# A time-mixing layer on one core: the first weight loaded between the halves of unit 0, and the scaling coefficients computed on rows

## The chip, the cores and the metric

The kernel runs on one core of one Trainium2 chip. The metric is the device time of one execution in microseconds; the time of a kernel is the median of its runs. The profile is one execution on the chip, taken by the hardware profiler; its span runs from the first to the last instruction.

## The reference

`x` has 16 sequences of 2048 tokens with 256 features each. Three per-feature mixing vectors and four 256 x 256 weights belong to it. Of these the key branch is computed by the reference and never used, so that the output is:

```python
x_prev[:, 1:, :] = x[:, :-1, :]          # the token before, zero for the first
xv = x * time_mix_v + x_prev * (1 - time_mix_v)
xr = x * time_mix_r + x_prev * (1 - time_mix_r)
v = xv @ value_weight
r = xr @ receptance_weight
out = (1 / (1 + np.exp(-r)) * v) @ output_weight
```

## The kernel before

**Tiling.** The work is cut into units of 512 tokens (`TU`), four of them in a sequence (`UB`), 64 in all. A unit holds four tiles (`UJ`) of 128 tokens; 256 features are two blocks (`KO`) of 128 partitions. For each unit TensorE transposes the tokens, so that the features lie on partitions (or a DMA transpose does it, for the last sequences). The transposed tokens stand in `xt`, where one more slot ahead of them holds the token before.

**The mixing.** The factor of a feature is moved into the weight: with `tms` = time_mix, `c_sb` = 1 / time_mix - 1 and the weight rows scaled by `tms`, the mixed input is `x + c_sb * x_prev` (`scale`, `add`). A zero in time_mix is replaced by 1e-30 first (line 241). For the receptance branch of unit 0 alone there is no mixing: `project_unmixed` adds up four products instead, two of the previous tokens with `w_prev` = weight * (1 - time_mix) and two of the tokens with the scaled weight `w_bf`.

**Per unit** follow the receptance product (`project` into `psum_r`), the sigmoid on ScalarE (`s_sb`), the value product (`psum_v`), the product of both on VectorE (`z_sb`), the output product (`psum_o`), and its copy and store. The main loop begins at line 646; the transposes of later units are put into it by `advance`.

**The order of the work** is written out by hand: each engine takes its instructions in the order in which the program names them, and only the semaphores between engines add to that. The start, which the change touches, runs like this:

- ScalarE's queue issues the two small loads of the mixing vectors into `tm_rows` (4 rows of 128, line 168). SP's queue issues, in this order, half 1 and half 0 of unit 0 (line 174), the receptance weight (line 180), half 1 and half 0 of unit 1, and the value weight (line 184). All six are 256 KB, in float32. Half 1 comes first since its last token column is the source of the shifted slot (line 309).
- GpSimd issues loads that cast to bfloat16: units 2 and 3 of sequence 0 (line 192), the first of them with a wait for the receptance weight; then the output weight (line 195) and sequence 1 in four pieces (line 152). Sequence 2 follows inside the loop (line 162).
- TensorE warms up on constants (line 204), transposes half 1 of unit 0 (line 300), then `tm_rows` (line 236, into a `psum_o` buffer), then half 0 in two parts of one tile, the second of them into the `psum_o` buffer again, and does a few more warm-up products.
- VectorE takes the four coefficients per partition out of PSUM (line 240) and works out `tms`, `tm_prev` and `c_sb` from them, five instructions on 128 x 4 elements (lines 241 to 249). Then it multiplies the first weight: `w_prev` (line 578, two instructions), the first block of `w_bf` (line 585). ScalarE does the second block (line 588), behind its copies of the transposed tokens (lines 305 and 309). Then VectorE mixes the value input of unit 0 (lines 354 and 376) and scales the value weight (line 594).
- TensorE's first products are those of line 398, then the transposes of unit 1 (line 272), the other half of `project_unmixed`, and the value product of unit 0 (line 384).

Of the kernel before, what the change touches and what calls it, by code (L numbers as in the profile page):

```python
# [8 lines left out]
FP32 = mybir.dt.float32  # L9
BF16 = mybir.dt.bfloat16  # L10
ALU = mybir.AluOpType
# [4 lines left out]
def kernel(  # L16
# [25 lines left out]
    nc = tc.nc  # L42

    B, S, D = x.shape
    P = 128
    KO = D // P
# [8 lines left out]
    H = UJ // 2  # L55
# [56 lines left out]
    loads = {}  # L112
# [51 lines left out]
    x_unit = opool.tile([P, 2, UJ, D], FP32, name="o_sb")  # L164
    tm_rows = consts.tile([2 * KO, P], FP32)
    w_f32 = consts.tile([P, 2, KO, D], FP32)
    for m, tm in enumerate([time_mix_r, time_mix_v]):
# [3 lines left out]

    def load_halves(e):
        for h in (1, 0):
            nc.sync.dma_start(  # L174
                out=x_unit[:, e, h * H : (h + 1) * H],
                in_=unit_rows(x, 0, e)[:, 0, h * H : (h + 1) * H, :],
            )

    load_halves(0)
    first_weight = nc.sync.dma_start(  # L180
        out=w_f32[:, 0], in_=receptance_weight.rearrange("(ko p) n -> p ko n", p=P)
    )
    load_halves(1)
    nc.sync.dma_start(out=w_f32[:, 1], in_=value_weight.rearrange("(ko p) n -> p ko n", p=P))
# [5 lines left out]
    x_first = xpool.tile([P, 2, UJ, D], BF16, name="x_bf")  # L190
    for e in (2, 3):
        op = nc.gpsimd.dma_start(out=x_first[:, e - 2], in_=unit_rows(x, 0, e)[:, 0])  # L192
# [36 lines left out]
    new_xt(0)  # L229
    tms = consts.tile([P, 2, KO], FP32)  # L230
    c_sb = consts.tile([P, 2, KO], FP32)
    tm_prev = consts.tile([P, 2, KO], FP32)

    def coefficients():
        ps = ps_o_pool.tile([P, 2, KO], FP32, name="psum_o")
        nc.tensor.transpose(
            out=ps.rearrange("p m k -> p (m k)"), in_=tm_rows, identity=ident_f[: 2 * KO, : 2 * KO]
        )
        tm = consts.tile([P, 2, KO], FP32)
        nc.vector.tensor_copy(out=tm, in_=ps)  # L240
        nc.vector.tensor_scalar(
            out=tms, in0=tm, scalar1=0.0, scalar2=1e-30, op0=ALU.is_equal, op1=ALU.mult
        )
        nc.vector.tensor_tensor(out=tms, in0=tms, in1=tm, op=ALU.add)
        nc.vector.tensor_scalar(
            out=tm_prev, in0=tm, scalar1=-1.0, scalar2=1.0, op0=ALU.mult, op1=ALU.add
        )
        nc.vector.reciprocal(c_sb, tms)
        nc.vector.tensor_scalar(out=c_sb, in0=c_sb, scalar1=-1.0, scalar2=None, op0=ALU.add)

# [44 lines left out]
    def first_transposes():  # L295
# [13 lines left out]
        nc.scalar.copy(out=xt[0][:, 0, :, 1:P], in_=ps[:, H - 1, :, 0 : P - 1])  # L309
        coefficients()  # L310
        part(0, 1, ps_v_pool, "psum_v")
        part(1, 1, ps_o_pool, "psum_o")

    def slots(piece, off=0):
# [260 lines left out]

    first_transposes()
    for ko in range(KO):
# [4 lines left out]
            scalar2=None,  # L582
# [166 lines left out]
```

## Time and profile before

| what | value |
|---|---|
| median of 3 runs | 199.56 us (198.65 to 200.79) |
| span of the profiled execution | 197.1 us; its own time beside the span isn't given |
| mean granted TensorE clock | 0.996 |
| busy TensorE / VectorE / ScalarE / GpSimd | 191.5 / 183.1 / 177.1 / 86.3 us |
| DMA moved | 58.13 MB, mean 295 GB/s |

How to read it: PE is TensorE's matmuls and PEld its weight loads, DVE is VectorE, ACT ScalarE, POOL GpSimd, SP the queue of SyncE; a `q` behind an engine is its instruction queue, as in SPq. L398 is line 398 of the kernel. In a timeline each row has its start, the time from the start of the first to the end of the last instruction that it merges, the engine, the line, the operation with its output and inputs, their shapes, and how many were merged; brackets hold the idle time of the engine ahead of it and whose work ended that. In the chain of waits a row is one link, with start and duration; "issue" is time in which nothing was waited for that the profile shows. In the table of DMA issues the last number is the time from the issue to the landing.

### The profile page before, as it was taken

Reading aid. Unit: us, or ns where it says so; the run is one execution under the profiler, and the core shown is the slowest. Engines: PE = TensorE matmul, PEld = TensorE weight load, DVE = VectorE, ACT = ScalarE, POOL = GpSimd, SP = SyncE. Lnnn points to the kernel's source line nnn. Section 1 sums busy time; section 2 is a strip of 40 time slices with the busy share of each in tenths; the row PEclk is TensorE's granted clock in tenths of the full one; section 3 lists DMA queues with packets and bytes.
Section 4 is the critical chain, followed back from the end, with each engine's and each line's share of the span. In section 5 each row is a group of like instructions: output and inputs, shape, how many; then the busy total and the mean of one; then the engine's idle time right before and its main releaser. Section 6 shows DMA issues by size and latency. Waiting matters only on the chain.

```text
span 197.1 us, 3735 instructions
## 1 busy us (share of the span) xinstructions
PE 191.5 (97%) x1358; PEld 123.0 (62%) x1364; DVE 183.1 (93%) x286; ACT 177.1 (90%) x197; POOL 86.3 (44%) x117
## 2 busy tenths in 40 slices
PE   8999999999999999999999999999999999999992
PEld 3556676666666666666666666666666666666660
DVE  0999999999999999999999999999999999999962
ACT  3699899999999999999999999999999999999982
POOL 2845542443665635624334266444433444444200
PEclk9999999999999999999999999999999999999998
DMA  5999999999999999999999999999999999999985
GB/s 185 238 176 224 218 254 262 247 259 262 296 413 283 283 296 332 283 238 198 376 209 290 335 346 186 212 218 241 290 290 419 419 421 419 416 416 421 382 327 221
DMA packets 35593, 58.13 MB, mean 295 GB/s; under 512 B 26004, under 2 KB 27128, under 8 KB 30840
## 3 DMA queue, kind: packets, MB, share of 16 engines
q1 hardware_dynamic: 31792, 41.34, 60.3%
q0 software_dynamic: 3632, 16.44, 41.6%
q8 instruction: 10, 0.16, 0.3%
q10 hardware_dynamic: 152, 0.13, 0.2%
q14 instruction: 7, 0.06, 0.1%
HBM read 34.34 MB, written 39.90 MB: 377 GB/s over the span
## 4 chain that ended last, share of the span: by engine, by line
PE 90%; DMA 6%; POOL 1%; issue 0%; SPq 0%; ACT 0%
PE psum_r L384 27%; PE psum_v L384 27%; PE psum_o L416 27%; PE ps_t L272 8%; DMA x_bf<-in_x_dram 4%; DMA w_f<-n_receptance_weight_dram 2%; PE ps_t L416 1%; POOL x_bf L192 1%; SPq L174 0%; POOL wo_bf L195 0%; PE psum_v L416 0%; POOL x_bf L152 0%; PE ps_t L384 0%; PE psum_r L416 0%; ACT x_bf L446 0%
## 5 line engine op out<-in xcount | busy, mean ns | idle before, releaser
L364 POOL TENSOR_SCALAR mix<-xt_both,c_sb 128x1024 bf16<-128x1024 bf16 (+1 forms) x55 | 61.1, 1110 | 85.5 <-DVE mix L376 82.3
L697 DVE TENSOR_TENSOR z_sb<-s_sb,psum_v 128x1024 bf16<-128x1024 bf16 (+1 forms) x64 | 76.8, 1201 | 2.3 <-PE psum_v L384 1.1
L376 DVE TENSOR_TENSOR mix<-mix,xt_both 128x1024 bf16<-128x1024 bf16 x112 | 76.8, 696 | 1.4
L384 PEld LDWEIGHTS <-w_bf 128*128 128x128 bf16 x512 | 48.5, 98 | 39.2 <-DVE mix L376 0.8
L658 ACT ACTIVATE s_sb<-psum_r 128x1024 bf16<-128x1024 f32 x63 | 65.2, 1034 | 6.2 <-PE psum_r L384 6.0
L384 PE MATMUL psum_v<-mix,w_bf 128*128 128x512 bf16 (+1 forms) x252 | 64.8, 378 | 0.4 <-DVE mix L376 0.2
L384 PE MATMUL psum_r<-mix,w_bf 128*128 128x512 bf16 x250 | 64.6, 379 | 0.2
L416 PE MATMUL psum_o<-wo_bf,z_sb 128*128 128x256 bf16 x486 | 63.2, 273 | 0.0
L416 PEld LDWEIGHTS <-z_sb 128*128 128x128 bf16 x512 | 52.0, 103 | 17.9 <-DVE z_sb L510 0.7
L471 ACT COPY o_sb<-psum_o 128x1024 f32<-128x1024 f32 x50 | 51.2, 1023 | 5.0 <-PE psum_o L416 4.8
L289 ACT COPY xt_both<-ps_t 128x1024 bf16<-128x1024 bf16 x32 | 32.9, 1039 | 0.0
L272 PEld LDWEIGHTS <-x_bf 128*128 128x128 bf16 x304 | 19.8, 98 | 8.4 <-DMA x_bf<-in_x_dram 0.4
L272 PE MATMUL ps_t<-ident,x_bf 128*128 128x128 bf16 x304 | 22.7, 219 | 0.2 <-DMA x_bf<-in_x_dram 0.2
L354 DVE TENSOR_SCALAR mix<-xt_both,c_sb 128x1024 bf16<-128x1024 bf16 (+1 forms) x47 | 21.3, 463 | 0.0
L638 ACT ACTIVATE mix<-xt_both,c_sb 128x1024 bf16<-128x1024 bf16 x14 | 16.3, 1163 | 0.0
L376 DVE TENSOR_TENSOR mix<-mix,xt_first 128x1024 bf16<-128x1024 bf16 x15 | 10.5, 708 | 0.1
L471 ACT COPY x_bf<-psum_o 128x1024 f32<-128x1024 f32 x10 | 10.2, 1015 | 0.0
L354 DVE TENSOR_SCALAR mix<-xt_first,c_sb 128x512 bf16<-128x512 bf16 x22 | 6.6, 350 | 0.3 <-ACT xt_first L282 0.2
L289 ACT COPY xt_first<-ps_t 128x1024 bf16<-128x1024 bf16 x6 | 6.0, 1022 | 0.0
L557 POOL COPY xt_first<-xt_first 128x254 bf16<-128x254 bf16 x5 | 2.0, 392 | 7.2 <-DVE mix L376 7.2
L162 POOL DMA_DIRECT2D x_bf<-in_x_dram x8 | 4.7, 584 | 0.0
L364 POOL TENSOR_SCALAR mix<-xt_first,c_sb 128x512 bf16<-128x512 bf16 x6 | 4.1, 685 | 1.3 <-DVE mix L376 0.8
(68 smaller groups left out, 52.3 us busy)
## 6 DMA issues: line engine op xcount, KB each, us to landing
out_dram<-o_sb SPq DMA_DIRECT2D x25, 1024.0 KB, 12.1
x_bf<-in_x_dram POOLq DMA_DIRECT2D x8, 1024.0 KB, 15.8
x_natural<-in_x_dram POOLq DMA_DIRECT2D x4, 1024.0 KB, 11.8
out_dram<-x_bf SPq DMA_DIRECT2D x4, 1024.0 KB, 14.4
x_natural<-in_x_dram POOLq DMA_DIRECT2D x4, 512.0 KB, 12.7
out_dram<-x_bf SPq DMA_DIRECT2D x4, 512.0 KB, 4.7
x_bf<-in_x_dram POOLq DMA_DIRECT2D x6, 256.0 KB, 7.0
o_sb<-in_x_dram SPq DMA_DIRECT2D x4, 256.0 KB, 3.9
```

The costliest lines, as they stand in the source:

```text
L162: return nc.gpsimd.dma_start(out=x_bf[b], in_=rows(b), max_dma_last_dim=run)
L272: nc.tensor.transpose(out=ps[:, jj], in_=src[:, jj, ko * P : (ko + 1) * P], identity=idn)
L289: nc.scalar.copy(out=xt[b][:, j0 : j0 + UJ], in_=ps)
L354: nc.vector.tensor_scalar(out=mixed(piece, ko), in0=tokens(piece, 0, ko), scalar1=c_sb[:, m, ko : ko + 1], scalar2=None, op0=ALU.mult,)
L364: op = nc.gpsimd.tensor_scalar(out=mixed(piece, 1), in0=tokens(piece, 0, 1), scalar1=c_sb[:, m, 1:2], scalar2=1.0, op0=ALU.mult, op1=ALU.mult,
L376: return nc.vector.tensor_tensor(out=mixed(piece), in0=mixed(piece), in1=tokens(piece, 1), op=ALU.add)
L384: nc.tensor.matmul(out=ps[:, mo, :], lhsT=w_bf[:, m, ko, mo * P : (mo + 1) * P], rhs=mixed((b, m, e * TU + lo, e * TU + hi), ko), start=(k ...
L416: nc.tensor.matmul(out=ps[:, j, :], lhsT=slot[:, ko, j], rhs=wo_bf[:, ko, :], start=(ko == 0), stop=(ko == KO - 1),)
L471: nc.scalar.copy(out=o[:, j0 : j0 + UJ, :], in_=ps)
L638: nc.scalar.activation(out=mixed(piece, ko), in_=tokens(piece, 0, ko), func=ACT.Copy, scale=c_sb[:, m, ko : ko + 1],)
L658: nc.scalar.activation(out=s_sb, in_=ps_r, func=ACT.Sigmoid)
L697: nc.vector.tensor_tensor(out=z_sb[:, :, c : c + n], in0=s_sb[:, :, c : c + n], in1=ps_v[:, :, c : c + n], op=ALU.mult,)
```

## The change

Three things are changed, all in the start.

- On SP's queue the receptance weight is issued between half 1 and half 0 of unit 0, no longer behind both.
- `tms` and `tm_prev` are computed on `tm_rows` itself, 4 rows of 128 (`row_s`, `row_prev`), ahead of the transpose. Then two small transposes, one for each, bring them to partitions, and one copy takes both out of PSUM (`coefs`, 128 x 8). Only the reciprocal follows at once; the subtraction of 1 that completes `c_sb` stands behind the scaling of the first weight.
- GpSimd's cast loads are issued by a function that is called after `first_transposes`; the first of them waits for the copy of the coefficients in place of the receptance weight.

```diff
+    coef_rows = [consts.tile([2 * KO, P], FP32, name=f"coef_rows{n}") for n in range(2)]
...
-    load_halves(0)
-    first_weight = nc.sync.dma_start(
+    load_half(0, 1)
+    nc.sync.dma_start(
         out=w_f32[:, 0], in_=receptance_weight.rearrange("(ko p) n -> p ko n", p=P)
     )
-    load_halves(1)
+    load_half(0, 0)
+    load_half(1, 1)
+    load_half(1, 0)
...
-    for e in (2, 3):
-        op = nc.gpsimd.dma_start(out=x_first[:, e - 2], in_=unit_rows(x, 0, e)[:, 0])
-        if e == 2:
-            tc.add_manual_dep(op.ins, first_weight.ins.name, SYNC, reason="behind the weight")
-    nc.gpsimd.dma_start(out=wo_bf, in_=output_weight.rearrange("(ko p) n -> p ko n", p=P))
-    load(1)
+
+    def cast_loads(after):
+        for e in (2, 3):
+            op = nc.gpsimd.dma_start(out=x_first[:, e - 2], in_=unit_rows(x, 0, e)[:, 0])
+            if e == 2:
+                tc.add_manual_dep(op.ins, after.ins.name, SYNC, reason="behind the first loads")
+        nc.gpsimd.dma_start(out=wo_bf, in_=output_weight.rearrange("(ko p) n -> p ko n", p=P))
+        load(1)
...
-    tms = consts.tile([P, 2, KO], FP32)
+    coefs = consts.tile([P, 2, 2, KO], FP32)
+    tms, tm_prev = (coefs[:, n] for n in range(2))
     c_sb = consts.tile([P, 2, KO], FP32)
-    tm_prev = consts.tile([P, 2, KO], FP32)
+    row_s, row_prev = coef_rows
+    nc.vector.tensor_scalar(
+        out=row_s, in0=tm_rows, scalar1=0.0, scalar2=1e-30, op0=ALU.is_equal, op1=ALU.mult
+    )
+    nc.vector.tensor_tensor(out=row_s, in0=row_s, in1=tm_rows, op=ALU.add)
+    nc.vector.tensor_scalar(
+        out=row_prev, in0=tm_rows, scalar1=-1.0, scalar2=1.0, op0=ALU.mult, op1=ALU.add
+    )
 
     def coefficients():
-        ps = ps_o_pool.tile([P, 2, KO], FP32, name="psum_o")
-        nc.tensor.transpose(
-            out=ps.rearrange("p m k -> p (m k)"), in_=tm_rows, identity=ident_f[: 2 * KO, : 2 * KO]
-        )
-        tm = consts.tile([P, 2, KO], FP32)
-        nc.vector.tensor_copy(out=tm, in_=ps)
...
+        ps = ps_o_pool.tile([P, 2, 2, KO], FP32, name="psum_o")
+        for n, row in enumerate(coef_rows):
+            nc.tensor.transpose(
+                out=ps[:, n].rearrange("p m k -> p (m k)"),
+                in_=row,
+                identity=ident_f[: 2 * KO, : 2 * KO],
+            )
+        op = nc.vector.tensor_copy(out=coefs, in_=ps)
         nc.vector.reciprocal(c_sb, tms)
-        nc.vector.tensor_scalar(out=c_sb, in0=c_sb, scalar1=-1.0, scalar2=None, op0=ALU.add)
+        return op
...
-    first_transposes()
+    cast_loads(first_transposes())
...
     nc.scalar.activation(
         out=w_bf[:, 0, 1, :], in_=w_f32[:, 0, 1, :], func=ACT.Copy, scale=tms[:, 0, 1:2]
     )
+    nc.vector.tensor_scalar(out=c_sb, in0=c_sb, scalar1=-1.0, scalar2=None, op0=ALU.add)
     scale(pieces(0)[1])
```

More of the change, by code (lines that the diff above doesn't have):

```diff
@@ L170, with load_half @@
         )
[L172 to L176, printed above, removed]
-            )
-    load_halves(0)
-    first_weight = nc.sync.dma_start(
+    def load_half(e, h):
+        nc.sync.dma_start(
+            out=x_unit[:, e, h * H : (h + 1) * H],
+            in_=unit_rows(x, 0, e)[:, 0, h * H : (h + 1) * H, :],
+        )
+    load_half(0, 1)
+    nc.sync.dma_start(
         out=w_f32[:, 0], in_=receptance_weight.rearrange("(ko p) n -> p ko n", p=P)
     )
-    load_halves(1)
+    load_half(0, 0)
+    load_half(1, 1)
+    load_half(1, 0)
     nc.sync.dma_start(out=w_f32[:, 1], in_=value_weight.rearrange("(ko p) n -> p ko n", p=P))
@@ L309, in first_transposes @@
         nc.scalar.copy(out=xt[0][:, 0, :, 1:P], in_=ps[:, H - 1, :, 0 : P - 1])
-        coefficients()
+        after = coefficients()
         part(0, 1, ps_v_pool, "psum_v")
         part(1, 1, ps_o_pool, "psum_o")
+        return after
     def slots(piece, off=0):
```

9 lines of the change are left out of this document (1 added, 8 removed).

## The prediction

> **What bounds the kernel now.** I read the page first: the engines' busy time and the chain that ended last.
>
> ```profile
> span 197.1 us, 3735 instructions
> PE 191.5 (97%) x1358; PEld 123.0 (62%) x1364; DVE 183.1 (93%) x286; ACT 177.1 (90%) x197; POOL 86.3 (44%) x117
> PE 90%; DMA 6%; POOL 1%; issue 0%; SPq 0%; ACT 0%
> ```
>
> TensorE is busy for 191.5 of 197.1 us and carries 90% of the chain. Another 7% of it is DMA and GpSimd, and the start is where one looks for that first. So the second view is the chain in order of time, over the first 25 us.
>
> ```profile
> 0.74 0.40 SPq L174
> ...
> 1.20 0.41 SPq L174
> ...
> 1.66 3.62 DMA w_f<-n_receptance_weight_dram
> 5.28 0.30 issue
> 5.58 0.74 POOL x_bf L192
> ...
> 6.33 0.55 POOL x_bf L192
> ...
> 8.12 7.37 DMA x_bf<-in_x_dram
> ```
>
> The receptance weight lands at 1.66 + 3.62 = 5.28. GpSimd, told to wait for it, begins its issues at 5.58: the two cast loads of unit 0's batch, then the output weight, then batch 1. The second load of batch 1, issued at 8.12, lands at 15.49. The chain then goes through TensorE without a long break, so what counts is when TensorE passes this point. The timeline there, and the two earlier waits of TensorE's path that matter, are the third view (start, duration, engine, line; in brackets the idle time before it and who ended it):
>
> ```profile
> 8.91 0.67 DVE L354 TENSOR_SCALAR mix<-xt_first,c_sb 128x512 bf16<-128x512 bf16 x2 [0.17 <-ACT xt_first L282]
> ...
> 12.10 0.55 PEld L384 LDWEIGHTS <-w_bf 128*128 128x128 bf16 x4 [0.42 <-DVE mix L376]
> ...
> 15.54 0.45 PEld L272 LDWEIGHTS <-x_bf 128*128 128x128 bf16 x8 [0.38 <-DMA x_bf<-in_x_dram]
> ```
>
> TensorE was ready at 15.54 - 0.38 = **15.16** and the data at **15.49**. Two chains meet here, 0.38 us apart: the load chain, which is late, and the compute chain, which has 0.38 us of slack. The compute chain can't win its slack back elsewhere: the wait at 12.10 is for VectorE's mixing, which itself began at 8.91 behind a ScalarE copy of TensorE's transposes of unit 1. A shift of those transposes therefore goes through to 15.16 one for one.
>
> **The start, row by row.** The fourth view is the timeline of the first 8 us.
>
> ```profile
> 3.66 0.98 PE L300 MATMUL psum_r<-ident_f,o_sb 128*128 128x128 f32 x4
> ...
> 4.57 0.23 PE L236 MATMUL psum_o<-ident_f,tm_rows 4*128 4x4 f32 x1
> 4.68 0.58 ACT L305 CAST xt_first<-psum_r 128x512 bf16<-128x512 f32 x1 [1.61 <-PE psum_r L300]
> ...
> 4.73 0.44 PE L300 MATMUL psum_v<-ident_f,o_sb 128*128 128x128 f32 x2
> 4.83 0.16 DVE L240 COPY tm<-psum_o 128x4 f32<-128x4 f32 x1 [3.96 <-PE psum_o L236]
> 5.03 0.17 DVE L241 TENSOR_SCALAR tms<-tm 128x4 f32<-128x4 f32 x1
> ...
> 5.05 0.44 PE L300 MATMUL psum_o<-ident_f,o_sb 128*128 128x128 f32 x2
> ...
> 5.23 0.16 DVE L244 TENSOR_TENSOR tms<-tms,tm 128x4 f32<-128x4 f32 x1
> 5.31 0.16 DVE L245 TENSOR_SCALAR tm_prev<-tm 128x4 f32<-128x4 f32 x1
> ...
> 5.42 0.39 ACT L305 CAST xt_first<-psum_v 128x256 bf16<-128x256 f32 x1
> 5.43 0.18 DVE L248 RECIPROCAL c_sb<-tms 128x4 f32<-128x4 f32 x1
> ...
> 5.65 0.17 DVE L249 TENSOR_SCALAR c_sb<-c_sb 128x4 f32<-128x4 f32 x1
> 5.68 0.41 ACT L305 CAST xt_first<-psum_o 128x256 bf16<-128x256 f32 x1
> 5.72 0.69 DVE L578 TENSOR_SCALAR w_prev<-w_f,tm_prev 128x256 bf16<-128x256 f32 x2
> 5.95 0.54 ACT L588 ACTIVATE w_bf<-w_f,tms 128x256 bf16<-128x256 f32 x1
> ...
> 6.14 0.73 PE L398 MATMUL psum_r<-xt_first,w_prev 128*128 128x512 bf16 x2 [0.26 <-ACT xt_first L305]
> 6.34 0.33 DVE L585 TENSOR_SCALAR w_bf<-w_f,tms 128x256 bf16<-128x256 f32 x1
> ...
> 6.60 0.65 DVE L354 TENSOR_SCALAR mix<-xt_first,c_sb 128x512 bf16<-128x512 bf16 x2
> ...
> 6.73 0.61 PE L398 MATMUL psum_r<-xt_first,w_bf 128*128 128x512 bf16 x2
> ...
> 7.17 1.04 PE L272 MATMUL ps_t<-ident_f,o_sb 128*128 128x128 f32 x8
> ```
>
> The first real product, at 6.14, was released by ScalarE's last copy of the transposed tokens (5.68 + 0.41 = 6.09), not by the weight: w_prev's first half (one of the two in 0.69 from 5.72) is done at about 6.07. Both inputs arrive within 0.02 us of each other; the later products of the group then wait for the scaled weights, the third until 6.73. The landing times come from the table of DMA issues, asked for one issue at a time (the last number is us from issue to landing); the row of queue 10, ScalarE's, is of the stretch 2.0 to 3.4 us.
>
> ```profile
> o_sb<-in_x_dram SPq DMA_DIRECT2D x1, 256.0 KB, 2.8
> ...
> o_sb<-in_x_dram SPq DMA_DIRECT2D x1, 256.0 KB, 3.4
> ...
> q10 hardware_dynamic: 4, 0.00, 0.3%
> ```
>
> Half 1 of unit 0 lands at 0.74 + 2.8 = 3.54, half 0 at 1.20 + 3.4 = 4.60, the weight at 5.28. The distances are 1.06 and 0.68.
>
> **Part 1, the weight between the halves.** One issue of 0.4 us and 256 KB changes places with another; no issue is added on SP's queue, and what follows (unit 1's halves, the value weight) keeps its place. All three are of one size, so I let the second in line land when the second did and the third when the third did: weight at 4.60 (0.68 earlier), half 0 at **5.28** (0.68 later). What the weight gains, the tokens lose, and the tokens released the first product. TensorE began 0.12 after half 1's landing (3.66), so it begins half 0 at 5.40. The first pair ends 0.44 later, at 5.84; the second pair starts 0.32 behind the first, as now (4.73, 5.05), at 5.72 and ends at 6.16. ScalarE copies the first pair from 5.88 and the second, 0.26 behind it (5.42, 5.68) but not before 6.18, for 0.41: the tokens are ready at **6.59**, the first product starts at 6.64, where it is 6.14 now. ScalarE's share of the weight scaling (L588), behind these copies, moves by the same half microsecond: from 6.45 to 6.99.
>
> **Part 2, coefficients on rows.** Three of VectorE's small instructions (L241, L244, L245: at 5.03, 5.23, 5.31, together 5.03 to 5.43) move ahead of the transpose, now on 4 rows. Both row vectors had been moved by 3.4 us, by queue 10's row, and VectorE is idle from its start to 4.83 (the 3.96 in brackets). Three instructions of 0.2 each end at about 4.0, ahead of the end of half 1's transposes (3.66 + 0.98 = 4.64): covered. If the rows came 0.6 us later, they would push the copy back one for one. The row shape (4 rows of 128) has no row in this trace; between 0.16 (these instructions) and 0.33 (L585, twice the width on all partitions), I take 0.2, and the cover holds at either end. Added on TensorE is a second small transpose, between 0 and 0.23 (L236's own, not overlapped); I take 0.2. So the copy starts at 5.03, twice as wide and still some 0.16, and ends at 5.19. The reciprocal follows 0.20 after its start, at 5.23, the w_prev products 0.08 behind that (as L245 behind L244): **5.31 instead of 5.72**, ready at 6.00; w_bf's first half at 6.26. The subtraction that finishes c_sb (0.17) moves behind them and ahead of the mixing of the value input (L354): that can start no earlier than the tokens, 6.64, where it starts at 6.60 now. VectorE's 0.41 is thus won and not used: the tokens are late next.
>
> The group's four products start at 6.64 and then every 0.22 (two take 0.61 or less, one of them 0.38): 6.86, 7.08, 7.30. The last needs ScalarE's weight half, ready at 6.99: no wait. Now the group has starts at 6.73 and 6.95 for its last two, since it waited. Unit 1's transposes follow at 7.52 instead of 7.17: **+0.35** for the compute chain, which reaches 15.16 + 0.35 = **15.51**. Bounds of this term: were half 0 to land as early as now, the chain would win about 0.1 (starts at 6.19, 6.41, 6.63, 6.85, none waiting); were the distance from weight to half 0 the 1.06 of the two halves, half 0 lands at 5.66 and the chain is 0.73 late.
>
> **Part 3, the cast loads behind the copy.** The wait moves from the weight's landing (5.28) to the copy's end (5.19). From the landing to the first issue passed 0.30; a wait for VectorE can cost between 0.05 and the same 0.30. So GpSimd begins at 5.24 to 5.49, 0.09 to 0.34 earlier than 5.58, and everything queued behind on GpSimd (two loads, the output weight, batch 1's four) moves along. If the transfers follow one for one, the data that TensorE waits for land at 15.15 to 15.40; if the DMA engines have no room, at 15.49 as now. TensorE starts 0.05 after landing: 15.20 to 15.54.
>
> **The sum.** TensorE starts the transposes at the later of 15.51 (compute) and 15.20 to 15.54 (load); now it is 15.54. That is **no change: -0.03 us**. From there TensorE runs to the end, so the span is 197.07. The profile gives no time of its own execution beside the span; the median of the runs, 199.56, lies 2.46 over the span, which nothing here changes. The forecast is 199.53, rounded **199.5**.
>
> **The rivals.**
> *A, the load chain decides.* If half 0 loses little by the swap, the compute chain is ready at 15.06 and the load chain's 0.09 to 0.34 is the gain: 199.2 to 199.5, middle 199.3. For it: the chain as it is drawn now goes through the weight and GpSimd, not through the tokens. Against it: 256 KB stand ahead of half 0 in one queue, and the first product waited for the tokens.
> The Trainium skill's page "SBUF — State Buffer", section "SBUF: two separate sides", says that GpSimd can't write the descriptors of its DMAs while VectorE runs an instruction that takes the shared port pair, as a scaling of SBUF data can. Here the two issues under VectorE's scalings took 0.74 and 0.55, so the trace allows 0.2 us of that; by the rule the earlier issues fall under the earlier w_prev scalings as they do now, and 0.2 of A's gain would be lost: 199.4.
> *B, slower: half 0 becomes the bound.* One mechanism: the tokens' transposes wait for half 0. It decides from the landing at which the compute chain passes 15.54, 0.03 later than I take, so from 5.31. At the distance of 1.06 (landing 5.66) the chain reaches 15.16 + 0.73 = 15.89: **+0.35**, 199.9; at 5.85, another 0.19: 200.1. For it: the trace has one distance of each size, and the transfer in the middle may be the slower for its shape. Against it: the last place in three ended at 5.28 whatever was in it.
> *C, the cast loads collide with the value weight.*
>
> ```profile
> 3.13 0.43 SPq L184 DMA_DIRECT2D w_f<-in_value_weight_dram  x1
> ...
> w_f<-in_value_weight_dram SPq DMA_DIRECT2D x1, 256.0 KB, 4.7
> ...
> 7.89 0.63 DVE L594 TENSOR_SCALAR w_bf<-w_f,tms 128x256 bf16<-128x256 f32 x2
> ```
>
> It lands at 7.83, and VectorE wants it at 7.89: 0.06 of cover. If the casts, 0.09 to 0.34 earlier, delay it by as much, VectorE is up to 0.28 late when it comes to the row at 8.91; but it waits 0.17 there now, and its input is 0.35 later after the change, so the delay is swallowed: 199.5.
> That the change doesn't do what it says is half of the forecast: w_prev is ready earlier, and nobody takes it.
>
> **How the numbers follow.** Forecast, with 0.15 us either way, 0.55; A 0.2; B 0.2; C 0.05. The mechanisms span -0.34 to +0.55: 199.2 to 200.1. The three runs of one kernel lie from 198.65 to 200.79, so a median carries some 0.6 us of its own; the range is **198.5 to 200.6**. No case comes near 1% (2.0 us, about what a measurement of this kernel can tell from no change), so only the runs' spread can: faster by more than that 0.04, slower 0.05 (B adds to it), within it 0.91.
>
> **What would show it.** Right: w_prev's multiplications start near 5.3; the copy of the last tokens ends near 6.6; the first product starts near 6.6, released by ScalarE, and the four follow without gaps; unit 1's transposes near 7.5; GpSimd's first issue near 5.3; the transposes of 15.54 within 0.15 of that. Wrong: half 0's transposes at 4.8 (then A), or at 5.7 and later (B); a row instruction still running at 4.6; and, for the whole, a TensorE that comes to 20 us with a shift that isn't found at the end of the span, since then something later has slack that I didn't see.

## The result, and the profile after

The changed kernel takes **201.04 us** (median of 10 runs, 199.33 to 202.13); before takes 199.23 (10 runs, 198.65 to 201.21). The ratio is **1.0075, 95% interval 1.0046 to 1.0104** (here and below it is a figure of its own, worked out with its interval, and not the quotient of the two medians): slower by three quarters of a percent, where no change was forecast, and the median is over the range of 198.5 to 200.6. Eight of the ten times lie from 200.9 to 202.1 and two near 199.35, while of before's ten eight lie below 199.6 and two near 201; the experiments call the times over 200.5 the upper group. The profiled execution is one of the two short ones (199.36 us, span 197.6), so its profile alone can't tell what the median lost. It is still the first thing to read.

The page of the changed kernel:

```profile
span 197.6 us, 3737 instructions
PE 191.9 (97%) x1359; PEld 123.1 (62%) x1365; DVE 183.6 (93%) x286; ACT 177.2 (90%) x197; POOL 86.5 (44%) x117
PE 93%; DMA 2%; DVE 1%; ACT 1%; issue 0%; POOL 0%; SPq 0%; POOLq 0%
```

DMA has gone from 6% to 2% of the chain, and VectorE and ScalarE have come into it: the loads of batch 1 no longer decide, the compute chain does. Its start, from the chain in order of time:

```profile
1.19 0.41 SPq L180
...
1.65 3.61 DMA o_sb<-in_x_dram
...
5.30 0.46 PE psum_v L307 x2
...
6.05 0.39 ACT xt_first L312
...
6.48 1.02 PE psum_r L406 x4
```

The chain now begins with half 0 of unit 0, behind the weight, and goes through ScalarE's last copy of the tokens, as the prediction had it. The timeline (line numbers of the changed kernel):

```profile
3.31 0.21 DVE L238 TENSOR_SCALAR coef_rows<-tm_rows 4x128 f32<-4x128 f32 x1 [2.44 <-DMA tm_rows<-in_time_mix_v_dram]
...
3.77 0.21 DVE L242 TENSOR_SCALAR coef_rows<-tm_rows 4x128 f32<-4x128 f32 x1
...
5.00 0.17 DVE L254 COPY coefs<-psum_o 128x8 f32<-128x8 f32 x1 [1.02 <-PE psum_o L249]
...
5.29 0.58 DVE L586 TENSOR_SCALAR w_prev<-w_f,coefs 128x256 bf16<-128x256 f32 x2
...
5.30 0.45 PE L307 MATMUL psum_v<-ident_f,o_sb 128*128 128x128 f32 x2 [0.34 <-DMA o_sb<-in_x_dram]
5.47 1.35 POOL L196 DMA_DIRECT2D x_bf<-in_x_dram  x2 [3.79 <-DVE c_sb L255]
...
6.05 0.38 ACT L312 CAST xt_first<-psum_o 128x256 bf16<-128x256 f32 x1
...
6.48 0.59 PE L406 MATMUL psum_r<-xt_first,w_prev 128*128 128x512 bf16 x2
...
6.91 0.59 PE L406 MATMUL psum_r<-xt_first,w_bf 128*128 128x512 bf16 x2
...
7.34 1.04 PE L279 MATMUL ps_t<-ident_f,o_sb 128*128 128x128 f32 x8
...
10.20 0.45 PEld L279 LDWEIGHTS <-x_bf 128*128 128x128 bf16 x8 [0.59 <-DMA x_bf<-in_x_dram]
...
14.73 1.09 PEld L279 LDWEIGHTS <-x_bf 128*128 128x128 bf16 x16
...
19.16 0.55 PEld L392 LDWEIGHTS <-w_bf 128*128 128x128 bf16 x4 [0.20 <-DVE mix L384]
...
144.97 1.22 DVE L706 TENSOR_TENSOR z_sb<-s_sb,psum_v 128x1024 bf16<-128x1024 bf16 x1 [0.38 <-issue]
```

Three rows were not foreseen. At 10.20 TensorE waits 0.59 for the **first** cast load; before, this load had landed at 9.35, and the same weight loads went ahead at 9.56 without a wait. At 19.16 it waits 0.20 for VectorE's mixing. And at 144.97 VectorE pauses 0.38 for nothing that the profile shows. The rows of before at the first and the third of these places:

```profile
9.56 0.65 PEld L272 LDWEIGHTS <-x_bf 128*128 128x128 bf16 x8
...
144.46 1.22 DVE L697 TENSOR_TENSOR z_sb<-s_sb,psum_v 128x1024 bf16<-128x1024 bf16 x1
```

Unit by unit, by the start of the sigmoid, the changed kernel is 0.23 behind at unit 2, 0.04 ahead at unit 3 (where before waits at 15.54 and this one doesn't: the row at 14.73 has sixteen weight loads in one), 0.15 behind from unit 5 to unit 47, and 0.45 behind from unit 48 to the end: 0.15 at the start and 0.30 from the pause make the 0.5 by which the spans differ. That leaves some 1.3 us of the median's 1.8 unexplained by this execution.

### The profile page after: what moved, and what is told of

Its sections match the earlier page's. It is cut to its first block, busy times and chain, and to the rows that moved or that the text cites. A ratio compares the mean times of both kernels' runs of the same rounds, so it can differ in the third digit from the quotient of the medians.

```text
span 197.6 us, 3737 instructions
## 1 busy us (share of the span) xinstructions
PE 191.9 (97%) x1359; PEld 123.1 (62%) x1365; DVE 183.6 (93%) x286; ACT 177.2 (90%) x197; POOL 86.5 (44%) x117
## 4 chain that ended last, share of the span: by engine, by line
PE 93%; DMA 2%; DVE 1%; ACT 1%; issue 0%; POOL 0%; SPq 0%; POOLq 0%
PE psum_v L392 28%; PE psum_r L392 27%; PE psum_o L424 27%; PE ps_t L279 8%; DMA o_sb<-in_x_dram 2%; PE ps_t L424 1%; DVE mix L384 1%; ACT xt_first L289 1%; PE psum_r L406 1%; DVE mix L362 0%; POOL mix L372 0%; ACT xt_first L312 0%; PE psum_v L424 0%; PE psum_v L307 0%; PE ps_t L392 0%
```

## The experiments

**1. The same kernel again, and the parts of the change.** The first theory for the long executions was TensorE's clock (theory 1); the rival was a late load (theory 2). Four kernels:

> The changed kernel once more. Its ten times lie in two groups, two near 199.35 and eight from 200.9 to 202.1; before has eight from 198.65 to 199.56 and two near 201. Theory 1 (clock): the upper group is an execution in which TensorE runs at half clock for one stretch more at the start, and the idle time of 0.33 us that TensorE now has while it waits for half 0 makes that likelier. Expected: mostly times of 200.9 to 201.5, and in a profile of that group the matmuls of 512 columns at the start take about twice their time for some 3.4 us, with TensorE about 1.7 us behind by 16 us. Theory 2 (data): the upper group is a late landing (half 0 or a cast load). Expected: the same times, but a profile in which a wait for a load grew by 1.7 us and the matmuls keep their length.

Measured: 200.95 (8 runs, 199.55 to 201.59), ratio 1.0080 (1.0049 to 1.0112). Its profile is of an execution of 200.69. TensorE's timeline in it:

```profile
5.36 0.69 PE L307 MATMUL psum_v<-ident_f,o_sb 128*128 128x128 f32 x2 [0.43 <-DMA o_sb<-in_x_dram]
...
7.01 1.06 PE L406 MATMUL psum_r<-xt_first,w_prev 128*128 128x512 bf16 x2
7.87 1.06 PE L406 MATMUL psum_r<-xt_first,w_bf 128*128 128x512 bf16 x2
...
9.64 0.59 PE L406 MATMUL psum_r<-xt_first,w_prev 128*128 128x512 bf16 x2
```

Two products take 1.06 where the short execution has 0.59 (rows at 6.48 and 6.91 above), until somewhere before 9.64. Unit 0 is 1.59 late, unit 5 1.46; the short execution was 0.17 late at unit 0, and half 0 landed only 0.05 later here, so that the clock costs some 1.4 us. So the clock does this in this execution, as theory 1 had it. The profile's own clock column reads full speed there, though the trace's first clock record, of full speed, lies at 8.80 (in the short execution at 4.92); the durations are what tells. The first cast load is late too (landed at 10.72), but TensorE comes to it at 11.15 and doesn't wait.

The order of the loads alone, on the kernel before:

```diff
...
-    load_halves(0)
+    load_half(0, 1)
     first_weight = nc.sync.dma_start(
         out=w_f32[:, 0], in_=receptance_weight.rearrange("(ko p) n -> p ko n", p=P)
     )
-    load_halves(1)
+    load_half(0, 0)
+    load_half(1, 1)
+    load_half(1, 0)
```

> The kernel before with the order of the loads alone changed: the first weight between the halves of unit 0; coefficients on partitions and the cast loads behind the weight as before. Theory 1: half 0 lands at about 5.3, TensorE idles for 0.3 to 0.4 us ahead of it, and most executions fall into the upper group: median near 201, ratio about 1.008. Theory 2: if the cast loads' place is what matters, the times stay with before, ratio 1.000 to 1.002.

Measured: 200.08 (12 runs, 198.81 to 201.79), ratio 1.0035 (1.0004 to 1.0066); four times over 200.5. Between the two theories, but the order alone is slower. Its profile is of the longest execution (201.79), with half 0 later than elsewhere (at 6.5) and TensorE idle for 1.80 us:

```profile
6.56 0.44 PE L301 MATMUL psum_v<-ident_f,o_sb 128*128 128x128 f32 x2 [1.80 <-DMA o_sb<-in_x_dram]
```

The granted clock by stages of 2 us (the column behind POOL's busy time) shows what followed:

```profile
7.00:9.00 2.00, 1.87 (x11) 0.79 (x9) 1.25 (x4) 1.05 (x3) 2.00 (x5) 0.67 0.92 159
9.00:11.00 2.00, 2.00 (x10) 1.80 (x9) 0.72 (x4) 0.51 (x1) 1.06 (x2) 0.50 0.94 149
```

The clock was taken back to half between 7 and 11 us after that idle time. The Trainium skill's page "TensorE: Matmul & The Clock Gate", section "Part 1: The HAM clock gate (the "warmup" mystery)", says that half speed is the default, that a window of about 3.4 us of activity lifts it, and that the windows run freely, so that the same kernel changes speed at another time from run to run. The traces agree: half speed lasts 3.41 us here (7.68 to 11.09), and full speed comes at 4.92 and at 8.80 in two executions of the changed kernel.

The changed kernel with the old order of the loads:

```diff
     load_half(0, 1)
+    load_half(0, 0)
     nc.sync.dma_start(
         out=w_f32[:, 0], in_=receptance_weight.rearrange("(ko p) n -> p ko n", p=P)
     )
-    load_half(0, 0)
```

> The changed kernel with the old order of the loads (half 1, half 0, weight); coefficients on rows and cast loads behind their copy stay. Theory 1: TensorE has no idle time ahead of half 0, most executions fall into the lower group: 198.6 to 199.3, ratio 0.998 to 1.000. Theory 2 with the cast loads as the cause: most stay in the upper group, ratio about 1.008.

Measured: 199.67 (12 runs, 199.51 to 200.58), ratio 1.0033 (1.0016 to 1.0050). The upper group is all but gone (one time), so it seems to come from the order; but the rest stands 0.55 over before, not below it: a miss, and the pause of VectorE is in this profile too (at 145.81).

The changed kernel with warm-up products in the gap:

```diff
         after = coefficients()
+        warm_up(4)
         part(0, 1, ps_v_pool, "psum_v")
```

> The changed kernel with four more warm-up products (one of 512 columns) between the transposes of the coefficients and those of half 0, so that TensorE is busy where it waits for half 0 now. Theory 1: most executions fall into the lower group, near 199.3, ratio about 1.000. Theory 2: nothing changes, most times stay at 200.9 to 201.5, ratio about 1.008.

Measured: 200.47 (9 runs, 199.99 to 201.71), ratio 1.0064 (1.0034 to 1.0094). Three of nine times over 200.5, in place of 14 of 18 in the two series of the changed kernel; but none is near 199.3. In its profile the clock is full early, and TensorE waits 0.94 us for the first cast load. So there is a second cause.

**2. Idle time, the pause, the rows.**

The kernel before with TensorE's second warm-up group (`warm_up(WARM2)`) removed:

> The kernel before without its second group of warm-up products (four, 0.56 us), nothing else changed: TensorE idles from about 5.5 to 6.1 while it waits for the tokens. Theory 1 (TensorE's idle time at the start decides in how many executions the full clock comes one stretch later): the upper group, 4 of 28 before, grows to about half or more; median 200 to 200.9, ratio 1.004 to 1.009, with the data and VectorE where they were. Theory 2 (the moved loads): nothing changes, ratio 1.000.

Measured: 199.26 (12 runs, 198.50 to 200.69), ratio 1.0021 (0.9993 to 1.0048); three times over 200.5, where before has 1 of 19 beside it. A miss: 0.52 us of idle time on TensorE at 5.92 costs next to nothing in most executions. But in this profile full speed had come at 5.54, ahead of that idle time; so the run shows that idle time there isn't enough to make an execution long, and not that the clock has no part in the upper group.

The changed kernel with as many listed instructions on VectorE as before:

```diff
-        (nc.vector if b == 0 else nc.gpsimd).memset(xt[b][:, 0, :, 0:1], 0.0)
+        nc.gpsimd.memset(xt[b][:, 0, :, 0:1], 0.0)
```

> The changed kernel with the small clearing of xt's first column on GpSimd in place of VectorE, so that VectorE has as many instructions as before. The profiles of all four kernels with coefficients on rows show a pause of 0.38 to 0.42 us on VectorE, at the same instruction (the product z_sb at about 145 us), and TensorE comes out of it 0.30 us later; the two kernels with coefficients on partitions don't have it. If it hangs on where that instruction stands in VectorE's stream: the pause is gone and the times fall by 0.3: the lower group near 199.05, the upper near 200.8. If it hangs on what the rows do: no change.

Measured: 200.10 (6 runs, 199.14 to 200.65), ratio 1.0055 (1.0035 to 1.0074). The product at this place follows without a wait:

```profile
145.74 1.22 DVE L706 TENSOR_TENSOR z_sb<-s_sb,psum_v 128x1024 bf16<-128x1024 bf16 x1
```

The lowest time fell by 0.2 (from 199.33 to 199.14). Over all profiles: the seven whose traces list 425 instructions for VectorE, waits for semaphores among them, have a pause of 0.37 to 0.39 between the 319th and the 320th, at 145.0 to 146.9 us, and TensorE comes out some 0.30 later in each; the eleven with 424 and the one with 421 (the mixing on ScalarE, below) don't have it. (In two of the seven the profile puts the pause down to a copy of ScalarE's that the product doesn't read; in five to nothing.) So it goes with the place in the stream: the clearing itself is on VectorE in before as well. That it is the fetch of instructions is only argued: the Trainium skill's page "Runtime: NRT & Kernel Launch", section "Instruction fetch mechanics", says that engines fetch their instructions in blocks of 256 and that crossing into the next is mostly hidden. Here one such pause would not be hidden, since VectorE is busy nearly without a break. But 320 is no multiple of 256, and no run shows the fetch itself.

The rows alone: `row_s`, `row_prev`, the two transposes and the later subtraction, with the old order and the casts behind the weight:

> Coefficients on rows alone; the loads in the old order and the casts behind the weight, as before. The kernel with rows and early casts in the old order was 0.55 us over before, 0.30 of it the pause of VectorE. Theory a: the rest (0.25) comes from the early cast loads, whose first landing has late engines: then this kernel has the pause alone, median 199.4, ratio 1.0015. Theory b: the rest comes from the second small transpose and the later tokens: median 199.65, ratio 1.003.

Measured: 199.60 (8 runs, 199.18 to 200.68), ratio 1.0043 (1.0022 to 1.0064): nearer to theory b. Yet its profile is 0.26 **ahead** of before from unit 5 to unit 35; then come a loss of 0.44 between units 35 and 40 (as large in no other profile) and the pause at 145.02.

Eight warm-up products in the gap, `warm_up(8)` in the same place:

> The changed kernel with eight warm-up products (two of 512 columns, 0.43 us at full clock, 0.85 at half) ahead of half 0's transposes. With four, 3 of 9 times were over 201, where the changed kernel had 11 of 18, but the others stood at 200 to 200.5 and not at 199.4, and its profile showed a wait of 0.94 us for the first cast load. Theory 1: no time over 201 but for those of late loads, median 200.2 or less, ratio 1.003 to 1.006. If the idle time isn't the cause: as the changed kernel, median 201, ratio 1.008 or more, since half 0's transposes come up to 0.5 us later.

Measured: 199.87 (6 runs, 199.37 to 200.90), ratio 1.0055 (1.0035 to 1.0075). No time over 201, as theory 1 has it, 1.1 below the changed kernel with the pause still in. In the profile TensorE has no gap ahead of half 0; what is left is a wait of 1.61 us of its weight loads for the first cast load.

**3. The first cast load.** The issue table gives the time from its issue to its landing. Before, and after:

```profile
x_bf<-in_x_dram POOLq DMA_DIRECT2D x1, 256.0 KB, 3.8
```

```profile
x_bf<-in_x_dram POOLq DMA_DIRECT2D x1, 256.0 KB, 4.7
```

In the profiles of before, after and all experiments, those further down too, it is, in us ("clearing moved" means that the clearing of `xt` is on GpSimd; so it is in the last four kernels of the left side, too):

| weight between the halves | | old order | |
|---|---|---|---|
| after; again; a third time | 4.7; 5.3; 3.9 | before | 3.8 |
| order only | 5.1 | rows and early casts | 4.2; 4.8 (clearing moved) |
| filled with 4; with 8; with 8, clearing moved | 6.2; 5.9; 6.1 | rows only | 4.4; 3.9 (clearing moved) |
| clearing moved | 6.4 | before without second warm-up | 3.7 |
| casts behind half 0 | 5.9 | rows, with the casts ahead of the moved clearing | 3.7 |
| weight in runs of 2 KB | 6.2 | | |
| mixing on ScalarE | 6.5 | | |
| casts behind the fourth load | 3.6 | | |

With the weight in the middle the casts' first load mostly takes 1 to 2.5 us longer, at moments of issue from 4.9 to 5.8 us: in ten of eleven such profiles it takes 4.7 or more, and 3.9 in the third look. Most of the load's 16 completions are on time and a few are late: in the short execution 14 come by 9.5, the last two at 10.14 and 10.16. Rivals for why: the early issue of the casts (theory L) or the order itself (theory M).

Rows alone once more, with the clearing on GpSimd:

> Coefficients on rows alone (old order of the loads, casts behind the weight), with the clearing of xt's first column on GpSimd, so that VectorE's stream has its old length. The profile of the rows alone was 0.26 us ahead of before from 20 to 115 us and lost it in pauses of VectorE's stream. If these are all that speaks against the rows: median 198.8, ratio 0.998 to 0.999. If the gain at the start was luck of one execution: 199.07, ratio 1.000.

Measured: 205.35 (6 runs, 204.93 to 205.93), ratio 1.0301 (1.0246 to 1.0356). A miss, and one of the experiment's own making: in this kernel the cast loads are issued ahead of the clearing in GpSimd's queue, and its first issue waits for the weight. The timeline:

```profile
10.38 0.18 POOL L233 MEMSET xt_first<- 128x2 bf16 x1
...
10.61 1.01 PE L408 MATMUL psum_r<-xt_first,w_prev 128*128 128x512 bf16 x2 [4.86 <-POOL xt_first L233]
```

TensorE waited 4.86 us for an instruction of 0.18 that stood behind seven DMA issues, and came out of it at half clock (two products in 1.01).

The kernel with rows and early casts in the old order, clearing on GpSimd:

> As the kernel above, but with the cast loads behind the coefficients' copy as in the changed kernel; the loads keep the old order. Theory L (it is the early issue of the casts, beside SP's loads, that makes the last engine of the first cast load late): first cast load complete at 10 or later, TensorE waits for it 0.5 us or more, median 199.6, ratio 1.003. Theory M (it is the order of the loads: the late landings, 10.16 to 11.56, stand in the five profiles with the weight in the middle, and 9.35 to 9.76 in the four with the old order): complete before 9.8, median 198.8 to 199.1, ratio 0.998 to 1.000.

Measured: 199.30 (12 runs, 198.61 to 200.63), ratio **0.9995 (0.9959 to 1.0030)**; without the clearing moved it was 199.67, ratio 1.0033. The first cast load is complete at 9.69 and TensorE doesn't wait for it (for the second it waits 0.60, at 12.03): theory M. The two kernels' ratios differ by 0.0038, some 0.76 us, more than the pause's 0.30; their intervals are wide enough for that. So two of the three parts of the change cost nothing that these runs can show, once VectorE's stream has its old length.

The changed kernel, clearing on GpSimd, casts behind half 0:

```diff
...
-    load_half(0, 0)
+    third_load = load_half(0, 0)
...
-    cast_loads(first_transposes())
+    first_transposes()
+    cast_loads(third_load)
```

> The changed kernel with the clearing on GpSimd (no pause of VectorE) and the cast loads behind the landing of half 0, the third load in line, in place of the coefficients' copy; the weight stays in the middle. Theory L: the casts no longer start beside half 0's transfer, the first is complete before 9.8, and the median falls from 200.1 to 199.3 or less. Theory M: still complete at 10 or later, median near 200.

Measured: 200.39 (12 runs, 199.39 to 201.25), ratio 1.0041 (1.0008 to 1.0074). The weight loads of TensorE:

```profile
11.37 0.45 PEld L279 LDWEIGHTS <-x_bf 128*128 128x128 bf16 x8 [1.83 <-DMA x_bf<-in_x_dram]
```

Still late (complete at 11.33): theory L, as put, falls. The profile is 0.10 behind at unit 0, 1.41 at unit 1 and 1.06 from unit 5 to the end, with the clock full from 4.14 on: this wait alone is worth about 1 us in it.

A third look at the changed kernel:

> The changed kernel once more, for a third profile of it. The first, of the fast group, had the full clock from 4.93 and waited 0.59 us for the first cast load at 10.2; the second, 1.3 us longer, had the full clock from 8.80 only. If late casts make the common time of 201: full clock by 5.5, a wait of 1 us or more for the first cast load near 10, and the time is 200.5 to 201.3. If the clock makes it: full clock from 8 us or later, and TensorE 1.5 us behind by 9 us.

Measured: 200.75 (8 runs, 199.87 to 201.53), ratio 1.0072 (1.0034 to 1.0110). The profile is of 201.26:

```profile
5.91 0.69 PE L307 MATMUL psum_v<-ident_f,o_sb 128*128 128x128 f32 x2 [1.03 <-DMA o_sb<-in_x_dram]
...
8.42 1.06 PE L406 MATMUL psum_r<-xt_first,w_bf 128*128 128x512 bf16 x2
```

The late clock again (full from 9.41), behind an idle second, and here the cast load is in time. Unit 0 is 2.17 behind, 2.0 more than in the short execution: 0.6 of it because half 0 landed later (5.87 in place of 5.26), the other 1.4 at half speed, as in the second look. So the two long executions of the changed kernel that were profiled are long through the clock, the second of them through half 0 as well, and in neither did TensorE wait for a cast load. The profiles in which it waited 0.9 us or more for the late cast load, with the clock full early, are of executions of 199.9 to 200.4, 0.8 to 1.3 us behind from unit 5 on. Both causes occur; the long times of this kernel, as far as two profiles tell, are the clock's.

**4. What the rows cost, and which part of the order does it.** The rows alone, with the clearing ahead of the cast loads on GpSimd:

> Coefficients on rows alone, old order of the loads, casts behind the weight, the clearing on GpSimd and now ahead of the cast loads in its queue: in the kernel tried before, it stood behind their issues, ran at 10.38, and TensorE waited 4.86 us for it. If the pauses of VectorE's stream are all that speaks against the rows: median 198.8, ratio 0.998 to 0.999. If the 0.26 us at the start were luck of one execution: 199.07, ratio 1.000.

Measured: 199.37 (12 runs, 198.71 to 200.72), ratio **0.9995 (0.9964 to 1.0026)**. Its profile is 0.16 ahead of before from unit 5 to the end, with no pause (span 196.9), and 198.71 is its time; the median shows no gain. So no cost of the rows is left without the pause, and the gain at the start is smaller than the runs can show.

The weight as 128 runs of 2 KB, with the clearing moved (the rows of the weight then stand in another order than the product wants, so the output isn't the reference's):

```diff
-    ... receptance_weight.rearrange("(ko p) n -> p ko n", p=P)
+    ... receptance_weight.rearrange("(p ko) n -> p ko n", p=P)
```

> The changed kernel with the clearing on GpSimd, and the receptance weight read in runs of 2 KB, two neighbouring rows on a partition (128 descriptors as for the tokens, in place of 256 of 1 KB); this leaves the weight's rows in another order than the product wants, so the values aren't the reference's. Theory M1 (the late engines of the first cast load come from the weight's many short runs in the second place): first cast load complete before 9.8, no wait near 10, median 199.5 or less. Theory M2 (they come from something else in the order): complete at 10 or later, median near 200.1.

Measured: 200.52 (12 runs, 199.43 to 201.34), ratio 1.0053 (1.0022 to 1.0084); first cast load complete at 11.30. The length of the weight's runs isn't it.

Filled gap and clearing moved:

> The changed kernel with eight warm-up products ahead of half 0's transposes and the clearing on GpSimd. If the two causes add up: 0.3 below the kernel with the eight products alone (199.87), so 199.55, ratio 1.002 to 1.004, no time over 201; what is left is the wait for the first cast load.

Measured: 199.81 (12 runs, 199.14 to 201.65), ratio 1.0035 (1.0003 to 1.0067). Within the expected ratio, 0.26 over the expected time; three times are over 200.5 and two of them over 201, so the fill doesn't make all executions alike; before, beside it, has 6 of 29 over 200.5. First cast load at 11.28, TensorE's products 0.46 late for it; half 0 landed at 5.93 here and makes unit 0 0.92 late.

The mixing products of unit 0 on ScalarE, clearing moved:

> The changed kernel with the clearing on GpSimd, and with the first two mixing products of unit 0's value input (L362) on ScalarE in place of VectorE. In seven of the nine profiles with a late first cast load, one of these products took 0.44 to 0.65 us where it takes 0.33 to 0.40 in the others, so VectorE and GpSimd may hold each other up there. Theory P: with VectorE idle at that time the first cast load is complete before 9.8. If it is complete at 10 or later again, VectorE's products are a victim and not the cause.

Measured: 200.62 (10 runs, 199.63 to 202.78), ratio 1.0059 (1.0033 to 1.0085); first cast load at 11.95, the latest of all, though VectorE was idle for 2.53 us up to 8.72. Theory P falls: VectorE's products aren't the cause.

The cast loads behind the fourth load, `fourth_load = load_half(1, 1)`, with the weight still in the middle and the clearing moved:

> The changed kernel with the clearing on GpSimd, and with the cast loads behind the landing of the fourth load (half 1 of unit 1, some 0.7 us after half 0), the weight still in the middle. Theory Q: the late engines come from the casts starting beside SP's transfers: then the first cast load is complete some 0.7 us later than on time at most (10.0 to 10.4), all engines within 0.6 us of the median one. If the last engine is 1.5 to 2.5 us behind the median one, as in the profiles of the changed order (median 8.8 to 9.2, last 10.2 to 11.6), it isn't SP's transfers.

Measured: 199.32 (10 runs, 198.83 to 201.15), ratio **1.0009 (0.9975 to 1.0043)**. The issue row of the first cast load, and TensorE's waits for half 0 and for that load:

```profile
x_bf<-in_x_dram POOLq DMA_DIRECT2D x1, 256.0 KB, 3.6
```

```profile
6.21 0.44 PE L307 MATMUL psum_v<-ident_f,o_sb 128*128 128x128 f32 x2 [1.20 <-DMA o_sb<-in_x_dram]
...
10.82 0.55 PEld L279 LDWEIGHTS <-x_bf 128*128 128x128 bf16 x8 [0.22 <-DMA x_bf<-in_x_dram]
```

Issued 1.7 us later than in the changed kernel (at 7.13), it lands in 3.6, at 10.8, with all its completions within 0.3 us of the median one, and the loss is gone as far as the interval tells. The profile itself is of one of the longer executions (200.13) and stands 1.16 behind at unit 0 already, because half 0 landed at 6.16 in it. This fits theory Q, that the late completions come from casts that start beside SP's transfers in this order, but doesn't show it: SP's last two loads were still under way (they landed at 7.54 and 8.20), and in the third look at the changed kernel the casts started at 5.40, beside the last four of SP's loads, and were in time. Why the same start is harmless in the old order stays open as well.

No kernel beats before beyond its interval; rows with early casts and rows alone (0.9995 each) equal it, as far as the intervals tell.

## Why the prediction was wrong, point by point

**The landings (Part 1) were right in the short execution, and taken as fixed where they scatter.** Half 0 was predicted at 5.28; there it was issued at 1.65 and the chain has it landed 3.61 later, at 5.26. Tokens ready: 6.59 predicted, 6.43 measured. First product: 6.64 and 6.48. Four products without a gap: right. Unit 1's transposes: 7.52 predicted, 7.34 measured, so the compute chain lost 0.17 where 0.35 was reckoned. (In the working, ScalarE's half of the weight is said to be ready at 6.45 before; its row, 5.95 + 0.54, gives 6.49, and the 6.99 after is worked out from that. Nothing hangs on it.) But in the changed kernel's second and third profiles half 0 landed at 5.31 and 5.87, and over all twelve profiles with the weight in the middle at 5.10 to 6.52, four times later than the 5.66 that rival B's first price was worked out from. The third load in line scatters as much in the old order, where it is the weight: 5.07 to 6.46 in seven profiles.

**The coefficients (Part 2) were right in the start and wrong behind it.** The rows were done at 3.98 (4.0 predicted), the copy began at 5.00 (5.03), w_prev at 5.29 (5.31), and nobody took that gain. The step that failed here is the pricing of VectorE's instructions by their durations alone. The page counts 286 busy instructions of VectorE before and after; but the trace lists 425 in place of 424, the one more being a wait for a semaphore ahead of the first row instruction, and a product at 145 us then paused 0.38. That is worth 0.30 us in the profiles, and the pause is gone in the three kernels whose clearing was moved to GpSimd (the changed kernel, the one with the old order, the rows alone). Their ratios fell by 0.0020, 0.0038 and 0.0048, which is 0.4 to 1.0 us: more than the pause explains, and not more than the intervals allow.

**The cast loads (Part 3): one consumer was priced, another paid.** The issue time was right (5.24 to 5.49 predicted, 5.47 measured), and the load of 15.5 indeed stopped deciding. But the part said "If the transfers follow one for one, the data that TensorE waits for land at 15.15 to 15.40; if the DMA engines have no room, at 15.49 as now", and priced no landing later than now, and only that one load. The first cast load, needed near 9.8, wasn't priced at all. It was complete at 10.2 in the short execution and at 10.7 to 12.0 in most others with this order. Where TensorE came to it on time, it waited 0.59 to 1.8 us. In the short execution the wait of 0.59 isn't on the chain and costs next to nothing (0.17 behind at unit 0, 0.24 at unit 1); where it is longer, it costs about 1 us at the end (200.1 to 200.4 with it, 199.3 with the casts behind the fourth load). Rival C may have had the right cause, casts beside SP's transfers, but had the wrong victim: the value weight landed at 7.54, in time.

**"From there TensorE runs to the end" was wrong by 0.15.** In the short execution TensorE was ahead at 16 us: its value product starts at 15.91 where it was 16.00, a little more than the forecast 0.03. VectorE, however, was still 0.23 late (15.78 against 15.55), has next to no slack of its own (93% busy), and made TensorE wait 0.20 at 19.16. Past the wait of 15.54 the prediction followed TensorE alone, and VectorE's chain decided.

**Not a term at all: the clock. As far as the changed kernel's profiles tell, this is the largest step that failed.** The sum assumed full clock from the start of the products, as the one profile had it. In three of the twelve profiles with the weight in the middle (the changed kernel's second and third, and the one with the mixing on ScalarE), TensorE ran at half speed until some 9 us and stood 1.6 to 2.2 us behind at unit 0; 1.4 to 1.5 of that is the clock, by the difference from the short execution less the later landing of half 0. With the pause's 0.30 and the 0.15 of the start that would make the median's 1.8. In none of the seven with the old order did full speed come so late; the rows alone with the casts ahead of the moved clearing lost it again, behind the wait of 4.86 us. The traces' first record of full speed lies at 8.80, 9.25 and 9.41 in these three and at 3.39 to 5.54 in the other sixteen; in the nine others with the weight in the middle it had come by 4.98, before half 0's transposes. So the gap ahead of half 0 seems to cost an execution the early full speed where that hasn't come yet; this is read from the profiles and was not tested by itself. The filled gaps indicate the same (20 of 26 times over 200.5 without, in three series, then 3 of 9, 1 of 6, 3 of 12). With the gap open and the clearing moved it is 1 of 6, 6 of 12 and 7 of 10 in three series; but with the casts behind the fourth load it is 1 of 10 with the gap open as well, so the gap alone doesn't decide. How the loss splits between the clock and the late loads over many executions isn't settled.

**The median and the span.** The 2.46 us that the prediction put around the span was too much: the changed kernel's profiled execution has 199.36 against a span of 197.6, 1.76. By that distance the profile of before was of an execution of some 198.9, shorter than the median of three then shown.

**Rival A** (the load chain decides) didn't come: in the short execution the load of batch 1 landed at 15.14, and TensorE came to it at 15.39.

**Rival B** (half 0 becomes the bound) named the right place in the chain and too small a set of consequences: its price of +0.35 was for the compute chain alone. In the changed kernel's third profile, with half 0 at 5.87, the later landing itself costs some 0.6.

## What to carry to other kernels

Swapping two equal loads in a queue gives one consumer what it takes from the other: find out first which of the two the next product really waits for. When GpSimd's casting loads are issued earlier, price every one of their consumers, not just the one that waits today, and price a later landing as well as an earlier one. Ask when TensorE's full clock comes, and what a new wait ahead of it may cost. And where an execution's times scatter by 1%, read more than one profile: none showed all of the causes.

## What the runs showed of the hardware that wasn't expected

- A casting load of 256 KB took 3.7 to 4.8 us from issue to landing in one order of the other queue's loads (seven profiles) and 4.7 to 6.5 in ten of eleven profiles with another, by a few late completions, with equal bytes and nearly equal times of issue.
- The third of six equal loads of one queue, issued at 1.65 in each, landed at 5.07 to 6.52 over nineteen profiles.
- VectorE paused 0.37 to 0.39 us ahead of the 320th of 425 listed instructions in seven traces, and in none of the twelve with 424 or 421.
- The granted clock in the profile read full speed over stages in which two 512-column products took 1.06 in place of 0.59. It fell to 0.50 in the two executions in which a full clock was taken back, behind 1.80 and 4.86 us of idle time on TensorE.
- An instruction of 0.18 us behind seven DMA issues on GpSimd cost the kernel 6 us, somewhat under a third of it through the clock.
